# Q·Kᵀ over 96 heads on one core: the later blocks hold eight heads instead of twelve

## The chip, the cores and the metric

The kernel runs on one core of a Trainium2 chip. The metric is the device time of one execution in microseconds (us), lower is better. Three executions of the kernel before gave 1061.80, 1062.16 and 1062.28 us; the median is 1062.16 us.

## The reference

For each of 8 × 12 = 96 heads, a 1024 × 64 matrix Q is multiplied with the transpose of a 1024 × 64 matrix K. Inputs and output are float32.

```python
def reference(q, k):          # q, k: (8, 12, 1024, 64), values 0.1 * randn
    return np.einsum('bhid,bhjd->bhij', q, k).astype(np.float32)   # (8, 12, 1024, 1024)
```

The inputs are 2 × 25.2 MB, the output is 402.7 MB: eight times as much is written as is read.

## The kernel before, in words

The 96 heads are cut into blocks of 2, 2, 4, 8, 8 and six times 12 heads (`sizes`). Within a block, each of Q and K goes through four steps, and then the heads are multiplied one by one.

1. **Load** (`Block.load`, L152 to L163). One DMA brings the float32 rows of all heads of the block into a buffer `x_sb`. Partition p takes the p-th part of the block's rows, which lies in one piece in HBM: 24 KB for twelve heads, 16 KB for eight. There are two `x_sb` buffers, and Q and K take turns, so the next block's Q goes where this block's Q was. Before the DMA is issued, the issuing engine waits until the casts have read the old contents. The loads of the blocks of 2 and 4 heads go to one of the output buffers instead, at the start.
2. **Cast** (`cast_quads`, the instruction at L211). GpSimd turns float32 into fp16, from `x_sb` into one of two buffers `half`. Each of Q and K makes two chunks, so a block has four chunks, and each chunk takes four instructions over 32 partitions.
3. **Transpose** (`transpose_quads`, L230). VectorE transposes a chunk in 32 × 32 squares from `half` into `qT` or `kT`. There are two pairs of `qT` and `kT`, used by blocks in turn. The first transpose of a block waits for the last matmul of the block two before it, which used the same pair. (The first two blocks are transposed by TensorE instead, L244.)
4. **Scores** (`Block.scores`). For each head, TensorE makes 8 × 2 matmuls of 64 × 128 by 64 × 512 (L312) into two halves of PSUM; ScalarE copies each half (128 × 2048 float32, L289) into one of three 4 MB output buffers `o_sb`, four copies a head; SyncE then waits for the fourth copy (L302) and issues one 4 MB store of the head, 32 KB for each partition. ScalarE's first copy into a buffer waits until the store that used the buffer three heads earlier has landed.

All engines' orders are written out by hand in `block()`, L391 to L414. While the heads of block i are multiplied, the four chunks of block i+1 are transposed, one in each quarter of the heads, and each transposed chunk frees a `half` for the next cast. During the same block, ScalarE's queue issues the two loads of block i+2: Q after the second copy of head `n` and K two heads later, where `LOADS` says which heads. Blocks of 12 issue at heads 6 and 8, blocks of 8 at heads 4 and 6, the block of 4 at heads 1 and 3. So the stores are on SyncE's DMA queue, and nearly all loads are on ScalarE's.

```python
    sizes = [2, 2, 4, 8, 8] + [12] * ((BH - 24) // 12)
    CHUNK, HALVES = 96 * 32, 2
    LOADS = {0: (), 1: (), 2: (1, 3), 3: (4, 6), 4: (4, 6)}
```

`CHUNK` is the size of a `half` buffer (elements in a partition), and `self.cut` (L142) is the number of pieces that half of a block's Q must be cut into to fit there; it is 1 in every block.

Of the kernel before, what the change touches and what calls it, by code (L numbers as in the profile page):

```python
# [6 lines left out]
F16 = mybir.dt.float16  # L7
F32 = mybir.dt.float32
P = 128
# [50 lines left out]
def kernel(  # L60
# [8 lines left out]
    B, H, S, D = q.shape  # L69
    NT = S // P  # L70
    BH = B * H
    assert D == 64 and NT == 8 and BH >= 36 and (BH - 24) % 12 == 0

    flat = [x.rearrange("b h s d -> (b h s) d") for x in (q, k)]
    of = out.rearrange("b h i j -> (b h) i j")

    sizes = [2, 2, 4, 8, 8] + [12] * ((BH - 24) // 12)
    PE_BLOCKS, EARLY = 2, 3
    NMAX = max(sizes)
    CHUNK, HALVES = 96 * 32, 2  # L80
    LOADS = {0: (), 1: (), 2: (1, 3), 3: (4, 6), 4: (4, 6)}

    pool = ctx.enter_context(tc.tile_pool(name="sb", bufs=1))
    psum = ctx.enter_context(
# [3 lines left out]
    x_sb = [pool.tile([P, NMAX * S * D // P], F32, name=f"x_sb{i}", tag=f"x{i}") for i in range(2)]  # L88
    half_sb = [pool.tile([P, CHUNK], F16, name=f"half{i}", tag=f"half{i}") for i in range(HALVES)]
    qk_sb = [  # L90
        [pool.tile([P, NMAX * S // 2], F16, name=f"{'qk'[x]}T{i}") for x in range(2)]
        for i in range(2)
    ]
    o_sb = [pool.tile([P, NT, S], F32, name=f"o_sb{i}", tag=f"out{i}") for i in range(3)]
# [27 lines left out]
    n, at = S * D // P * 2, 8 * S // 2  # L122
# [227 lines left out]
    def next_load(eng):  # L350
        if stream:
            b, x = stream.pop(0)
            assert b.i == EARLY or not any(i == b.i - 1 and c[0] == x for i, c in casts)
            b.load(x, eng)
# [20 lines left out]
    def to_half(last):  # L375
        while casts:
            i, c = casts[0]
            if i > last or (blocks[i], c[0]) in stream:
                return
            if not (rooms if i == PE_BLOCKS else halves).free():  # L380
                return
            done = blocks[i].cast_quads(*c)
            if i == 2:
                early_busy[:] = [done]
            casts.pop(0)

    def transposed(b, s):
        b.transpose_quads(*s)
        to_half(b.i)

    def block(i, heads, regions, w):  # L391
        b = blocks[i]
        nxt = blocks[i + 1] if i + 1 < len(blocks) else None
        for n in heads:
            side = {}
            if nxt and nxt.by_pe:
                if n == 1:
                    side = {
                        u: [
                            lambda x=u // 2: nxt.transpose_rows(  # L400
                                x, regions.next(), dve, nc.vector.tensor_copy
                            )
                        ]
                        for u in (1, 3)
                    }
            elif nxt:
                parts = nxt.chunks()
                some = [s for m, s in enumerate(parts) if m * b.N // len(parts) == n]
                side = {0: [lambda s=s: transposed(nxt, s) for s in some]}
            if n in LOADS.get(i, (6, 8)):  # L410
                side[1] = side.get(1, []) + [lambda: next_load(act)]
            b.scores(n, side, regions, w)
            to_half(i + 2 + (n == b.N - 1))
# [8 lines left out]
    for x in range(2):  # L422
        blocks[0].transpose_rows(
            x, quarters.next(), (dve, act)[x], (nc.vector.tensor_copy, nc.scalar.copy)[x]
        )
        to_half(2)
    block(0, [0], quarters, 1)
    halves_ps = Ring([ps_all[:, 2 * S :], ps_all[:, : 2 * S]])
    halves_ps.busy = [quarters.busy[2] + quarters.busy[3], quarters.busy[0] + quarters.busy[1]]
    block(0, [1], halves_ps, 2)  # L430
    for i in range(1, len(blocks)):
        block(i, range(blocks[i].N), halves_ps, 2)
# [31 lines left out]
```

## Time and profile before

| | before |
|---|---|
| time, median of three | 1062.16 us (1061.80 to 1062.28) |
| profiled execution, its span | 1060.4 us (the profile lists no other time of it) |
| TensorE matmul busy | 700.5 us (66%) |
| ScalarE busy | 697.0 us (66%) |
| VectorE busy | 470.6 us (44%) |
| GpSimd busy | 345.3 us (33%) |
| moved by DMA | 453.19 MB, mean 427 GB/s |
| read from and written to HBM | 50.33 MB, 402.65 MB |

The profile is of one execution. Its engines are PE (TensorE), DVE (VectorE), ACT (ScalarE), POOL (GpSimd) and SP (SyncE, which only issues DMAs here); a q behind the name means the engine's own sequencer, for instance while it issues a DMA. The DMA rows count 16 DMA engines that all transfers share: a share of 1.00 or tenths of 9 mean that all sixteen hold a packet nearly all the time. A DMA's packet here is one partition's piece, and q1 and q10 are the queues of SyncE and ScalarE. Behind the DMA rows the trace has a record of each packet (queue, start, duration, size), and of the small completion write that each of the 16 engines makes at the end of each DMA; where the text speaks of packet records, it means these.

### The profile page before, as it was taken

The page shows a single profiled execution, that of the slowest core. Times are in us where ns is not written, and L with a number is a line of the kernel's source. Part 1 is how long each engine was busy: PE and PEld are TensorE (multiplying, and loading weights), DVE is VectorE, ACT ScalarE, POOL GpSimd, SP SyncE. Part 2 cuts the span into 40 slices and gives each one's busy share as a digit, 9 for nine tenths or more (in the row PEclk, how much of TensorE's full clock was granted, in tenths as well). Part 3 has the DMA queues.
Part 4 walks back from the last instruction along what each step waited for, and adds up shares of the span by engine and source line. Part 5 has one row for each costly group of instructions (what it writes and reads, how often), then busy time and mean ns, then how long its engine had stood idle before and what let it go on. Part 6 is the DMA issues. An engine that isn't in the chain of part 4 may idle for free.

```text
span 1060.4 us, 3258 instructions
## 1 busy us (share of the span) xinstructions
PE 700.5 (66%) x1568; PEld 127.3 (12%) x800; DVE 470.6 (44%) x43; ACT 697.0 (66%) x386; POOL 345.3 (33%) x158
## 2 busy tenths in 40 slices
PE   6876755765577557774577855777557777778770
PEld 2111100110111001110011100111001111111110
DVE  2998602991795006960069600795007950000000
ACT  4766755755678557775577755776557777777771
POOL 7667216436360430704307053160531600000000
DMA  9999999999999999999999999999999999999997
GB/s 376 434 435 434 432 419 430 435 428 431 433 432 428 428 435 430 430 431 423 438 431 429 433 431 434 434 429 422 426 432 435 429 434 434 434 435 430 431 434 336
DMA packets 17583, 453.19 MB, mean 427 GB/s; under 512 B 1952, under 2 KB 1952, under 8 KB 2976
## 3 DMA queue, kind: packets, MB, share of 16 engines
q1 hardware_dynamic: 14976, 410.00, 90.0%
q10 hardware_dynamic: 2592, 42.99, 9.7%
q8 instruction: 9, 0.15, 0.0%
q14 instruction: 6, 0.05, 0.0%
HBM read 50.33 MB, written 402.65 MB: 427 GB/s over the span
## 4 chain that ended last, share of the span: by engine, by line
DMA 71%; ACT 17%; PE 7%; DVE 2%; issue 1%; POOL 0%; ACTq 0%; SPq 0%
DMA out_dram<-o_sb 70%; ACT o_sb L289 17%; PE ps_all L312 7%; DVE kT L230 1%; DVE qT L230 1%; DMA o_sb<-in_q_dram 0%; PE ps_all L244 0%; POOL qT L180 0%; DVE kT L251 0%; ACT kT L251 0%; ACTq L36 0%; SPq L168 0%; SPq L459 0%; SPq L97 0%
## 5 line engine op out<-in xcount | busy, mean ns | idle before, releaser
L289 ACT COPY o_sb<-ps_all 128x2048 f32<-128x2048 f32 (+1 forms) x384 | 694.7, 1859 | 333.0 <-DMA out_dram<-o_sb 301.6
L312 PE MATMUL ps_all<-kT,qT 64*128 64x512 f16 x1536 | 696.4, 617 | 327.8 <-ACT o_sb L289 322.4
L211 POOL CAST half<-x_sb 32x3072 f16<-32x3072 f32 (+1 forms) x128 | 323.4, 2527 | 491.6 <-DMA x_sb<-in_q_dram 242.2
L230 DVE STREAM_TRANSPOSE qT<-half 128x3072 f16<-128x3072 f16 (+1 forms) x16 | 222.9, 14132 | 370.0 <-PE ps_all L312 370.0
L309 PEld LDWEIGHTS <-qT 64*128 64x128 f16 x768 | 124.2, 162 | 896.8 <-issue 889.2
L230 DVE STREAM_TRANSPOSE kT<-half 128x3072 f16<-128x3072 f16 (+1 forms) x16 | 224.2, 14217 | 2.8 <-POOL half L211 2.8
L230 DVE STREAM_TRANSPOSE kT<-kT 128x1024 f16<-128x1024 f16 x2 | 9.3, 4836 | 0.0
L230 DVE STREAM_TRANSPOSE qT<-qT 128x1024 f16<-128x1024 f16 x2 | 9.2, 4784 | 0.0
L211 POOL CAST qT<-o_sb 32x1024 f16<-32x1024 f32 x8 | 8.3, 1034 | 1.2 <-DMA o_sb<-in_q_dram 0.8
L211 POOL CAST kT<-o_sb 32x1024 f16<-32x1024 f32 x8 | 8.3, 1033 | 0.5
L251 DVE COPY qT<-ps_all 128x1024 f16<-128x1024 f16 x2 | 2.5, 1225 | 11.0 <-PE ps_all L244 11.0
L289 DVE COPY o_sb<-ps_all 128x1024 f32<-128x1024 f32 x4 | 4.9, 1225 | 4.4 <-PE ps_all L312 4.4
L244 PE MATMUL ps_all<-ident,qT 128*128 128x128 f16 x16 | 2.1, 310 | 6.7 <-POOL qT L180 6.6
L251 ACT COPY kT<-ps_all 128x1024 f16<-128x1024 f16 x1 | 1.0, 1012 | 4.7 <-PE ps_all L244 4.7
L180 POOL CAST qT<-o_sb 128x512 f16<-128x512 f32 x4 | 2.3, 612 | 3.6 <-DMA o_sb<-in_q_dram 3.6
L251 DVE COPY kT<-ps_all 128x1024 f16<-128x1024 f16 x1 | 1.2, 1225 | 4.4 <-PE ps_all L244 4.4
L251 ACT ACT_TABLE_LOAD x1 | 1.3, 1283 | 2.8 <-issue 2.8
L244 PE MATMUL ps_all<-ident,kT 128*128 128x128 f16 x16 | 2.0, 305 | 0.7 <-ACT o_sb L289 0.7
L180 POOL CAST kT<-o_sb 128x512 f16<-128x512 f32 x4 | 2.3, 613 | 0.4 <-DMA o_sb<-in_q_dram 0.4
L244 PEld LDWEIGHTS ps_all<-ident,qT 128*128 128x128 f16 x16 | 1.5, 140 | 6.9 <-POOL qT L180 6.9
L244 PEld LDWEIGHTS ps_all<-ident,kT 128*128 128x128 f16 x16 | 1.5, 136 | 3.3 <-POOL qT L211 1.6
L359 POOL MEMSET ident<- 128x128 f16 x1 | 0.2, 205 | 0.5 <-SPq L97 0.5
(5 smaller groups left out, 0.7 us busy)
## 6 DMA issues: line engine op xcount, KB each, us to landing
out_dram<-o_sb SPq DMA_DIRECT2D x96, 4096.0 KB, 21.7
x_sb<-in_q_dram ACTq DMA_DIRECT2D x6, 3072.0 KB, 22.0
x_sb<-in_k_dram ACTq DMA_DIRECT2D x6, 3072.0 KB, 21.9
x_sb<-in_q_dram SPq DMA_DIRECT2D x1, 2048.0 KB, 14.6
x_sb<-in_k_dram SPq DMA_DIRECT2D x1, 2048.0 KB, 19.6
x_sb<-in_q_dram ACTq DMA_DIRECT2D x1, 2048.0 KB, 18.3
x_sb<-in_k_dram ACTq DMA_DIRECT2D x1, 2048.0 KB, 19.1
o_sb<-in_k_dram ACTq DMA_DIRECT2D x4, 256.0 KB, 4.7
```

Of the source, the lines that this page charges most:

```text
L180: lambda: nc.gpsimd.tensor_copy(out=rows[:, :, h], in_=self.raw[x][:, h * n : (h + 1) * n].rearrange("p (r d) -> p r d", d=D),),
L211: lambda: nc.gpsimd.tensor_copy(out=dst[q0 : q0 + 32].rearrange("p (r d) -> p r d", d=32), in_=raw[32 * b : 32 * b + 32, c * m : (c + 1) * ...
L230: lambda: nc.vector.transpose(out=dst, in_=buf.rearrange("p (r i) -> p r i", i=32)),
L244: lambda: nc.tensor.transpose(t_ps[:, t], rows[:, t], ident),
L251: lambda: copy(out=dst, in_=t_ps.rearrange("c t m -> c m t")), [done]
L289: lambda: (nc.vector.tensor_copy if by_dve else nc.scalar.copy)(out=dst, in_=ps[:, : w * S]),
L309: return nc.tensor.ldweights(stationary, tile_position=(at, 0))
L312: return nc.tensor.add_instruction(mybir.InstMatmult(name=nc.get_next_instruction_name(), ins=[nc.tensor.lower_ap(moving), nc.tensor.lower ...
L359: cleared = gps.run(lambda: nc.gpsimd.memset(ident, 0.0))
```

## The change

All blocks behind the first three hold eight heads: 2, 2, 4 and then eleven times 8. Loads in blocks of 8 go on being issued at heads 4 and 6, which is now the rule for all of them. The buffers `x_sb` and `half` shrink with the largest block; the buffers of `qT` and `kT` keep their size for twelve heads, since the early blocks use their back part as working space (`rooms`).

```diff
-    assert D == 64 and NT == 8 and BH >= 36 and (BH - 24) % 12 == 0
+    assert D == 64 and NT == 8 and BH >= 24 and BH % 8 == 0
...
-    sizes = [2, 2, 4, 8, 8] + [12] * ((BH - 24) // 12)
+    sizes = [2, 2, 4] + [8] * ((BH - 8) // 8)
     PE_BLOCKS, EARLY = 2, 3
     NMAX = max(sizes)
-    CHUNK, HALVES = 96 * 32, 2
-    LOADS = {0: (), 1: (), 2: (1, 3), 3: (4, 6), 4: (4, 6)}
+    CHUNK, HALVES = 64 * 32, 2
+    LOADS = {0: (), 1: (), 2: (1, 3)}
...
     qk_sb = [
-        [pool.tile([P, NMAX * S // 2], F16, name=f"{'qk'[x]}T{i}") for x in range(2)]
+        [pool.tile([P, 12 * S // 2], F16, name=f"{'qk'[x]}T{i}") for x in range(2)]
...
-            if n in LOADS.get(i, (6, 8)):
+            if n in LOADS.get(i, (4, 6)):
                 side[1] = side.get(1, []) + [lambda: next_load(act)]
```

## The prediction

> **What bounds the kernel now.** I began with the DMA rows of the page, because the busy shares of the engines (66% at most) name no bound.
>
> ```profile
> DMA  9999999999999999999999999999999999999997
> DMA packets 17583, 453.19 MB, mean 427 GB/s; under 512 B 1952, under 2 KB 1952, under 8 KB 2976
> q1 hardware_dynamic: 14976, 410.00, 90.0%
> q10 hardware_dynamic: 2592, 42.99, 9.7%
> DMA 71%; ACT 17%; PE 7%; DVE 2%; issue 1%; POOL 0%; ACTq 0%; SPq 0%
> ...
> out_dram<-o_sb SPq DMA_DIRECT2D x96, 4096.0 KB, 21.7
> x_sb<-in_q_dram ACTq DMA_DIRECT2D x6, 3072.0 KB, 22.0
> ...
> x_sb<-in_q_dram ACTq DMA_DIRECT2D x1, 2048.0 KB, 18.3
> x_sb<-in_k_dram ACTq DMA_DIRECT2D x1, 2048.0 KB, 19.1
> ```
>
> The sixteen DMA engines are full from the first slice to the last: 90.0% for the queue of the stores (and the first loads), 9.7% for the other loads. The chain of waits, in a stretch without and one with loads, says what each costs:
>
> ```profile
> 334.91 29.09 DMA out_dram<-o_sb
> ...
> 371.55 29.21 DMA out_dram<-o_sb
> ...
> 408.60 21.21 DMA out_dram<-o_sb
> ...
> 891.20 21.72 DMA out_dram<-o_sb
> ...
> 920.47 21.72 DMA out_dram<-o_sb
> ```
>
> One step is three heads, because there are three output buffers. Late, without loads, it takes 920.47 - 891.20 = 29.27 us, 9.76 us for a 4 MB store. From 334.91 to 408.60, two steps with one 3 MB load each, it is 73.69 us, so two loads cost 73.69 - 58.54 = 15.15 us. A store lands 21.7 us after its issue, over two store times, so the queue holds another store whenever one ends. Time is made of what the DMA engines do per byte, per DMA and in slow packets; nothing else counts until it empties that queue.
>
> **The change part by part.** The change of instructions does what its words say: 18 loads of 16 KB a partition stand where 12 of 24 KB were (blocks 5 to 10 become 5 to 13); matmuls, copies and stores are the same in number, and SyncE's order is unchanged.
>
> *Bytes.* 12 × 3 MB = 18 × 2 MB. Nothing.
>
> *Six more DMAs, 768 more packets.* The packet records give 1213 ns as the commonest duration of a 32 KB packet, 912 ns for 24 KB, 611 ns for 16 KB. That is linear, with some 9 ns a packet beyond the bytes. On each of 16 engines, 12 × 8 × 912 ns = 87.6 us becomes 18 × 8 × 611 ns = 88.0 us: +0.4 us. The spacing of completion writes includes the DMA's end: 9.68 us for a 4 MB store, and 4.89 us for a 2 MB load at the start. Twice the second less the first is 0.10 us for each DMA whatever its size, hence +0.6 us for six. I take +0.6, which is measured on whole DMAs; +0.4 is the low end. As to the high end, the 256 KB loads land 4.7 us after issue; if each added load stood alone and held everything for that time it would be 28 us. It cannot be so while the queue is full, as at these loads.
>
> The Trainium skill, "DMA: Bandwidth & Descriptors", section "Anatomy of one DMA", speaks against the change: it fits a DMA (on GpSimd's path) as about 2.0 us fixed plus its bytes over 436 GB/s; by that, an estimate is 6 × 2.0 = 12 us more if the fixed part were paid in line. The trace disagrees as long as the queue is full: 0.10 us a DMA.
>
> *Slow packets.* Some packets take 60 to 1200 ns over the commonest duration of their size, and they crowd into the first 10 us of a load, of Q above all, in the load's own and in the stores' packets. Summed over both queues and divided by 16 engines, the six pairs of 3 MB loads (from 140, 240, 340, 480, 600 and 740 us) have 0.7, 0.4, 0.7, 0.8, 0.4 and 1.0 us, 4.0 us in all. The one pair of 2 MB loads that runs beside stores, 60 to 120 us, has 0.08 us. The windows over such pairs and over a free stretch show the same, roughly:
>
> ```profile
> 62.50:111.50 49.00, 31.37 (x71) 5.56 (x35) 45.09 (x6) 30.07 (x17) 36.98 (x21) 1.00 1.00 433
> 345.50:399.50 54.00, 28.96 (x66) 5.19 (x32) 0.00 (x0) 29.08 (x16) 21.92 (x8) 1.00 1.00 430
> 610.00:664.00 54.00, 29.06 (x64) 5.20 (x32) 0.00 (x0) 29.20 (x17) 21.92 (x8) 1.00 1.01 433
> 862.00:1030.00 168.00, 125.26 (x277) 22.37 (x138) 1.15 (x1) 123.60 (x68) 0.00 (x0) 1.00 1.00 432
> ```
>
> (Last columns: share of the DMA engines, GB/s.) If 16 KB pieces have no slow packets, -4.0 us; if they come once for each pair, nine pairs instead of six make +2.0; if they go by bytes, 0. But the end is not set by the mean engine. The sixteen completion writes of the last store are spread over 5.3 us, and the last engine is one that has lost about 0.08 us in every store of the load-free stretch, while it lost only some 0.9 us over all six load stages beyond that. On this engine the ends are -0.9 and +0.45 us. I take 0: one pair of 2 MB loads is thin evidence for none, and the early pair on SyncE's queue (20 to 40 us, no stores beside) has 0.6 us of slow packets at 16 KB.
>
> *Casts, transposes, issues.*
>
> ```profile
> L211 POOL CAST half<-x_sb 32x3072 f16<-32x3072 f32 x96 | 263.0, 2740 | 467.4 <-DMA x_sb<-in_q_dram 238.6 <-DVE qT L230 224.0
> L230 DVE STREAM_TRANSPOSE kT<-half 128x3072 f16<-128x3072 f16 x12 | 187.0, 15797 | 0.0
> L211 POOL CAST half<-x_sb 32x2048 f16<-32x2048 f32 x32 | 60.4, 1887 | 24.3 <-DVE qT L230 13.0 <-DMA x_sb<-in_k_dram 6.1 <-DMA x_sb<-in_q_dram 3.5
> L230 DVE STREAM_TRANSPOSE qT<-half 128x2048 f16<-128x2048 f16 x4 | 37.3, 9503 | 1.1 <-PE ps_all L312 1.1
> ```
>
> And the list of waits:
>
> ```profile
> ACT o_sb L289 <- DMA out_dram<-o_sb: 301.6, 89, 8.3
> ```
>
> POOL: 176 × 1.887 = 332 us instead of 323. DVE: 44 × 9.49 = 418 us instead of 447. Both lie beside stores: a block of eight lasts 8 × 9.68 + 2 × 4.89 = 87 us, its four transposes 4 × 9.5 = 38 us, its sixteen casts 30 us, so the next block is ready some 49 us early; cover gone, POOL's +9 us would be the price. ACT issues six more loads at 0.33 us (its row), 2 us, beside 301.6 us in which it waits for stores; uncovered, +2. The wait before an issue is for casts that ended long before: the last cast of K follows the block's second transpose (19 us) and takes 7.5 us, so it is over 27 us into the block, and K's load comes at head 6, some 60 us in. Queued behind that wait are ACT's copies, for which PE and then SyncE's stores wait; none of it moves. Q's load, 18 us to landing, is through when K's is issued 24 us later; K's lands about 2 us into the next block, where its first transpose comes 19 us in. Late next, if anything, is that K. Smaller `x_sb` and `half` free SBUF that nothing uses: nothing.
>
> *Sum.* The profiled span, 1060.4 us, is 1.8 us under the median of the runs, which I keep as what lies around the span. 1060.4 + 0.6 + 0 = 1061.0 us of span, so 1062.8 us.
>
> **The rivals.**
>
> *A, the forecast: all hidden.* Full queue, +0.6 us, slow packets as before on the engine that ends last: 1062.8, between 1061.5 (no slow packets, low price: +0.4 - 0.9) and 1063.6. For it: the shares of 1.00 in all windows. Against: it hangs on the one slow engine staying the last.
>
> *B, faster: 16 KB pieces have no slow packets, and all engines gain.* -4.0 + 0.6 = -3.4 us: 1058.8. For it: 0.08 against 0.4 to 1.0 us a pair. Against: a single pair, and the last engine has only 0.9 us to give. It decides from 2.7 us of recovered time on the last engine, which needs that engine's steady loss to be smaller in the timed runs than in the profiled one.
>
> *C, slower, the other side: slow packets come with each load's beginning.* Nine pairs instead of six, on the engine that ends last as on the mean one: +2.0 + 0.6 = 2.6 us: 1064.8. It decides from 1.5 us more in slow packets. For it: they crowd at the beginnings of loads. Against: the 2 MB pair.
>
> *D, slower: a new wait empties the queue of stores.* The place is the first matmul of a block, which waits for the transposes. When a store lands, two more are queued, 19.4 us, and refilling the freed buffer takes 1.9 + 1.9 + 3.6 = 7.4 us in the chain, so the stores run 12 us ahead. If K came late by more than the 49 + 12 = 61 us, each of the nine blocks would lose the rest: 1 us each gives 1071.8. For it: a block has a third less time. Against: its work shrinks likewise, and the eight-head block that stands in the trace has no such wait.
>
> *E, slower: the fixed part of a DMA is paid.* A 256 KB load lands 4.7 us after its issue, and its 8 packets on an engine take 8 × 84 ns = 0.7 us; if the sixteen engines stood still for the other 4.0 us at each of six added loads, it would be 24 us: 1086.8 with A's 0.6. Every window with loads has a DMA share of 1.00, which is against it. By the Trainium skill's figure above, in place of this one, it would be about 1074.
>
> **How the numbers follow.** A 0.48, B 0.26, C 0.18, D 0.06, E 0.02. The prediction is A's, 1062.8 us. A's own range is 1061.5 to 1063.6. The range reaches to B's and C's times with the 0.2 us by which the two prices of a DMA differ, 1058.6 to 1065.0, and leaves out D, E and the outer parts of B and C. Within 0.2% of the median, 2.1 us, is what cannot well be told from no change: A is there (0.48); faster is B (0.26); slower are C, D and E (0.26).
>
> **What would show it.** Right: q10 with 768 more packets of data (and 96 completion writes) at about the same share; a DMA share of 1.00 in windows over every pair of loads; a late three-head step of 29.3 us; two steps with a load each at about 58.5 + 9.8 us; casts and transposes over long before their block starts. B would show as slow packets of less than 1 us over all nine later pairs of loads; C as 6 us; D as long waits of PE for DVE at L312; E as slices of the DMA row below 9. I am wrong if the slow packets have another cause than the loads' shape, for instance the place in HBM, which moves with the blocks too, or if the slow engine of this execution is not there in others.

## The result, and the profile after

The changed kernel takes 1066.29 us (median, 1065.72 to 1067.06) beside 1062.22 us before in the same comparison: a ratio of 1.0037, 95% interval 1.0025 to 1.0048, or +4.1 us with +2.7 to +5.1 as its interval. The forecast was no change (1062.8 us); the time lies 1.3 us above its range, which ended at 1065.0 us, and 1.5 us above rival C's 1064.8 us. The profiled execution has a span of 1064.6 us (before: 1060.4), and its own time is 1066.41 us, so 1.8 us lie around the span again.

The page of the changed kernel, its DMA rows (the columns are as before):

```profile
DMA  9999999999999999999999999999999999999997
GB/s 374 433 433 434 434 433 430 433 419 432 432 429 422 437 434 425 432 433 414 430 433 424 426 433 433 422 432 434 425 425 432 424 429 432 431 433 433 433 433 316
q1 hardware_dynamic: 14976, 410.00, 89.9%
q10 hardware_dynamic: 3456, 42.99, 9.6%
...
x_sb<-in_q_dram ACTq DMA_DIRECT2D x10, 2048.0 KB, 19.7
x_sb<-in_k_dram ACTq DMA_DIRECT2D x10, 2048.0 KB, 19.7
```

The engines are full as before, the bytes are the same, and q10 has 864 more records: 768 packets of data and 96 completion writes. Only the rate dips, more often than before, to 414 to 426 GB/s.

The chain of waits (start and length in us), two steps with a load each and late ones without:

```profile
394.77 26.64 DMA out_dram<-o_sb
...
428.96 26.98 DMA out_dram<-o_sb
...
463.50 21.48 DMA out_dram<-o_sb
...
895.24 21.50 DMA out_dram<-o_sb
...
924.30 21.50 DMA out_dram<-o_sb
...
953.35 21.48 DMA out_dram<-o_sb
982.38 23.00 DMA out_dram<-o_sb
1012.94 21.41 DMA out_dram<-o_sb
```

A step without loads is 29.06 us, 0.2 us less than the 29.27 us before, which fits with the engine that was last before and lost 0.08 us in each store. The step from 982.38 to 1012.94 is an exception, 30.56 us; more on it below. The two steps with loads take 463.50 - 394.77 = 68.73 us, so two loads cost 10.6 us for 9.6 us of bytes (8 × 602 ns for each at the packets' slope). Nine later pairs pay such a surplus instead of six.

The groups of instructions and the waits:

```profile
L211 POOL CAST half<-x_sb 32x2048 f16<-32x2048 f32 x176 | 332.1, 1887 | 547.5 <-DMA x_sb<-in_q_dram 348.8
L230 DVE STREAM_TRANSPOSE qT<-half 128x2048 f16<-128x2048 f16 x22 | 204.1, 9466 | 463.4 <-PE ps_all L312 463.4
```

```profile
ACT o_sb L289 <- DMA out_dram<-o_sb: 305.8, 89, 6.3
PE ps_all L312 <- DVE kT L230: 3.0, 1, 3.0
```

Casts cost what was worked out (332 us), transposes a little less (410 us in their two rows, instead of 418), and no block waits for them: PE's matmuls wait for these transposes once, 3.0 us, in this kernel and in the one before. Rival D, a new wait, is out, and so is E.

Windows of 50 us over the early pair of 2 MB loads, over four of the nine later pairs, and a late stretch without loads (last columns: DMA share, GB/s):

```profile
62.50:111.50 49.00, 31.44 (x71) 5.59 (x35) 45.10 (x6) 30.09 (x17) 36.95 (x21) 1.00 1.01 434
...
310.00:360.00 50.00, 29.06 (x65) 5.19 (x32) 8.03 (x1) 29.09 (x17) 15.09 (x8) 1.00 1.00 426
...
488.00:538.00 50.00, 29.41 (x66) 5.32 (x33) 9.31 (x2) 29.45 (x17) 15.09 (x8) 1.00 1.01 424
...
752.00:802.00 50.00, 29.64 (x67) 5.29 (x33) 8.89 (x1) 29.68 (x17) 15.09 (x8) 1.00 1.00 425
840.00:890.00 50.00, 29.07 (x65) 5.18 (x32) 8.21 (x1) 29.11 (x17) 15.09 (x8) 1.00 1.00 424
910.00:1040.00 130.00, 97.10 (x215) 17.15 (x106) 8.74 (x1) 97.04 (x54) 0.00 (x0) 1.00 1.00 433
```

The early pair loses nothing, in this kernel too; the four later pairs shown, of the same 2 MB loads, lose about 2%, and the other five 1 to 2% (424 to 429 GB/s).

**Where the 4.2 us of span went.** The packet records give three terms. The slow packets (all that packets of both queues took beyond the commonest duration of their size, divided by 16) rose from 6.1 to 8.6 us over the whole run, +2.5 us; behind the first 60 us of the records, where the later loads are, from 4.7 to 7.4 us. The mean of the sixteen completion writes of the last store came 2.9 us later (1051.2 us behind the first load's completion before, 1054.2 after), which leaves 0.4 us for the six added DMAs. And the last of the sixteen engines was 5.0 us behind the mean one instead of 3.5: +1.5 us. Together 4.4 us; the span grew by 0.2 us less, since less of it lies behind the last completion.

Most of the third term does not come from a load. In the store ahead of 982 us the last engine was 3.8 us behind the mean one, 0.3 us more than at the end of the kernel before. The step at 982 us, with no load near, takes 30.56 us where its neighbours take 29.03 to 29.06, and the packet records have one instruction fetch at 981.84 us: a single packet of 16 KB, 961 ns long, on one of the sixteen engines. The kernel before has its fetch at 978.56 us, but its steps show nothing of it:

```profile
979.02 21.72 DMA out_dram<-o_sb
1008.30 21.72 DMA out_dram<-o_sb
```

So the fetch there ran on an engine that was not the last. Such a long step about 980 us, 1.4 to 1.7 us over its neighbours, stands in seven of nine profiles with 18 loads (this one and eight from the experiments below) and in none of the four with 12 (at most 0.8 us there). Whether that is chance is not shown.

### The profile page after: what moved, and what is told of

Its sections match the earlier page's. It is cut to its first block, busy times and chain, and to the rows that moved or that the text cites. A ratio compares the mean times of both kernels' runs of the same rounds, so it can differ in the third digit from the quotient of the medians.

```text
span 1064.6 us, 3333 instructions
## 1 busy us (share of the span) xinstructions
PE 700.6 (66%) x1568; PEld 127.3 (12%) x800; DVE 432.7 (41%) x55; ACT 697.1 (65%) x386; POOL 353.9 (33%) x206
## 4 chain that ended last, share of the span: by engine, by line
DMA 71%; ACT 17%; PE 7%; DVE 2%; issue 1%; POOL 0%; ACTq 0%; SPq 0%
DMA out_dram<-o_sb 71%; ACT o_sb L289 17%; PE ps_all L312 7%; DVE kT L230 1%; DVE qT L230 1%; DMA o_sb<-in_q_dram 0%; PE ps_all L244 0%; POOL qT L180 0%; DVE kT L251 0%; ACT kT L251 0%; ACTq L36 0%; SPq L168 0%; SPq L459 0%; SPq L97 0%
## 5 line engine op out<-in xcount | busy, mean ns | idle before, releaser
L211 POOL CAST half<-x_sb 32x2048 f16<-32x2048 f32 x176 | 332.1, 1887 | 547.5 <-DMA x_sb<-in_q_dram 348.8
L230 DVE STREAM_TRANSPOSE qT<-half 128x2048 f16<-128x2048 f16 x22 | 204.1, 9466 | 463.4 <-PE ps_all L312 463.4
L230 DVE STREAM_TRANSPOSE kT<-half 128x2048 f16<-128x2048 f16 x22 | 205.9, 9551 | 2.9 <-POOL half L211 2.9
## 6 DMA issues: line engine op xcount, KB each, us to landing
x_sb<-in_q_dram ACTq DMA_DIRECT2D x10, 2048.0 KB, 19.7
x_sb<-in_k_dram ACTq DMA_DIRECT2D x10, 2048.0 KB, 19.7
```

Source lines behind the costliest of these rows:

```text
L211: lambda: nc.gpsimd.tensor_copy(out=dst[q0 : q0 + 32].rearrange("p (r d) -> p r d", d=32), in_=raw[32 * b : 32 * b + 32, c * m : (c + 1) * ...
L230: lambda: nc.vector.transpose(out=dst, in_=buf.rearrange("p (r i) -> p r i", i=32)),
```

## The experiments

Each kernel was measured beside the kernel before on the same chip. "Slow" is the sum of slow packets behind the first 60 us, and "mean end" and "last" are the mean engine's end and how far the last engine is behind it, all three from the packet records of one profiled execution. Loads are counted that begin beside stores, behind the early pair.

| kernel | later loads × piece | slow, us | mean end, us | last, us | time, us | ratio, 95% interval |
|---|---|---|---|---|---|---|
| before | 12 × 24 KB | 4.7 | 1051.2 | 3.5 | 1062.4 | |
| changed | 18 × 16 KB | 7.4 | 1054.2 | 5.0 | 1066.3 | 1.0025 to 1.0048 |
| changed, again | 18 × 16 KB | 6.6 | 1054.0 | 6.6 | 1066.4 | 1.0025 to 1.0050 |
| pair at once | 18 × 16 KB | 7.2 | 1054.1 | 6.0 | 1066.5 | 1.0028 to 1.0053 |
| same place | 18 × 16 KB | 7.5 | 1054.1 | 4.0 | 1065.5 | 1.0023 to 1.0048 |
| 16 KB, 24 KB apart | 18 × 16 KB | 7.6 | 1054.6 | 4.8 | 1066.3 | 1.0020 to 1.0046 |
| 16 KB, 17 KB apart | 18 × 16 KB | 7.6 | 1054.9 | 4.9 | 1067.2 | 1.0031 to 1.0061 |
| GpSimd busy | 18 × 16 KB | 7.7 | 1054.5 | 4.0 | 1066.0 | 1.0024 to 1.0055 |
| VectorE busy | 18 × 16 KB | 6.2 | 1053.3 | 5.0 | 1065.9 | 1.0022 to 1.0049 |
| changed, early loads | 18 × 16 KB | 7.3 | 1054.2 | 4.9 | 1066.3 | 1.0024 to 1.0051 |
| before, loads behind stores | 12 × 24 KB | 4.9 | 1051.8 | 4.2 | 1064.9 | 1.0014 to 1.0032 |
| 24 KB, 32 KB apart | 12 × 24 KB | 5.1 | 1051.3 | 4.0 | 1062.4 | 0.9988 to 1.0008 |
| before, early loads | 12 × 24 KB | 4.8 | 1051.8 | 3.4 | 1062.9 | 0.9994 to 1.0012 |
| blocks of ten | 14 × 20 KB | 5.8 | 1052.7 | 3.8 | 1064.3 | 1.0006 to 1.0024 |
| blocks of six | 24 × 12 KB | 7.9 | 1054.7 | 3.4 | 1065.5 | 1.0024 to 1.0049 |
| loads in two halves | 36 × 8 KB | 5.9 | 1053.3 | 4.9 | 1065.5 | 1.0018 to 1.0044 |
| blocks of four | 38 × 8 KB | 4.7 | 1052.4 | 6.1 | 1065.0 | 1.0017 to 1.0037 |

**Do the slow packets come where reading begins?** The first theory, rival C made sharper, was that each stretch of reading beside stores pays once.

```diff
-            if n in LOADS.get(i, (4, 6)):
-                side[1] = side.get(1, []) + [lambda: next_load(act)]
+            loads = LOADS.get(i, (4, 4))
+            if n in loads:
+                side[1] = side.get(1, []) + [
+                    lambda: next_load(act) for _ in range(loads.count(n))
+                ]
```

> The changed kernel, but K's load is issued right behind Q's at head 4 instead of two heads later: nine pairs of loads make nine stretches of reading beside stores instead of eighteen. Theory S (slow packets come where reading begins, about 0.39 us for each beginning, from 6.9 us over 18 later loads in the changed kernel's packet records): nine beginnings fewer, -3.5 us against the changed kernel, about 1062.8 us. Rival D (each DMA pays its own beginning, back to back or not): 1066.3 us. Rival Y (slow packets go by bytes read): 1066.3 us, too, with the slow packets spread over the whole of the loads.

Nothing was won: 1066.5 us. The page of this kernel shows that the loads did follow one another, K landing 15 us behind Q:

```profile
x_sb<-in_q_dram ACTq DMA_DIRECT2D x10, 2048.0 KB, 20.0
x_sb<-in_k_dram ACTq DMA_DIRECT2D x10, 2048.0 KB, 34.7
```

So it is not the stretch of reading that pays; eighteen loads in nine stretches have as many slow packets (7.2 us) as in eighteen. The plain theory falls. (The pause that this run takes away is short, since Q landed 19.7 us after its issue and K was issued about 24 us after Q; the opposite case, Q and K four heads apart, is below.)

```diff
-    sizes = [2, 2, 4] + [8] * ((BH - 8) // 8)
+    sizes = [2, 2, 4, 8] + [4] * ((BH - 16) // 4)
...
-    LOADS = {0: (), 1: (), 2: (1, 3)}
+    LOADS = {0: (), 1: (), 3: (4, 6)}
...
-            if n in LOADS.get(i, (4, 6)):
+            if n in LOADS.get(i, (1, 3)):
```

> Blocks of 2, 2, 4, 8 and then twenty times 4: 40 loads of 1 MB (8 KB a partition) on ScalarE's queue where the changed kernel has 20 of 2 MB. Theory S: 20 more beginnings at 0.39 + 0.10 us, +9.7 us against the changed kernel, about 1076 us. Rival Y (by bytes): only 20 x 0.10 us more, 1068.3 us.

1065.0 us, under both numbers and far under the theory's. A load of 8 KB pieces has only 0.09 us of slow packets on the mean engine, against 0.37 us for the 16 KB pieces of the changed kernel and 0.32 us for the 24 KB pieces of the one before. (These prices per load count packets over 60 ns too slow, from 3 us before a load's first packet to 1 us behind its last.)

**Is it the two queues taking turns?** The loads of block 5 and later go to SyncE's queue, between stores.

```diff
-                side[1] = side.get(1, []) + [lambda: next_load(act)]
+                side[1] = side.get(1, []) + [lambda: next_load(sp if i >= EARLY else act)]
```

> The kernel before (blocks of 12), but the loads of block 5 and later are issued on SyncE's queue, between two stores, instead of on ScalarE's: no two queues to take turns between. Theory S in its plain form (a read that begins beside running stores costs something, from whatever queue): 1062.2 us, as before. Rival Q (the slow packets come from taking turns between two queues): the 4.0 us of slow packets over the six pairs are gone on the mean engine, about 1058 to 1060 us.

```profile
x_sb<-in_q_dram SPq DMA_DIRECT2D x6, 3072.0 KB, 29.3
x_sb<-in_k_dram SPq DMA_DIRECT2D x6, 3072.0 KB, 36.7
```

The loads now wait their turn (29 and 37 us to landing instead of 22), and the slow packets stay, 4.9 us. Rival Q falls. The time even rose, to 1064.9 us; the profiled execution took 1063.3 us, the lowest time of this kernel, and its records do not show where the other 1.6 us of the median lie. That is left open.

**Is it the place, or the distance of the pieces?** First, every load of block 5 and later reads block 4's rows.

```diff
-            src = flat[x][self.first * S : (self.first + self.N) * S]
+            first = min(self.first, blocks[4].first) if self.i > 4 else self.first
+            src = flat[x][first * S : (first + self.N) * S]
```

> The changed kernel, but every load of block 5 and later reads the rows of block 4 (heads 8 to 15) again, whose own loads had no slow packets; so the output from head 16 on is that of other heads. Theory S: 1066.3 us, slow packets as in the changed kernel. Rival P (the place in HBM decides): slow packets fall to about 0.1 us a pair, -6 us, about 1060 us.

7.5 us of slow packets and 1065.5 us, so the place does not decide. Second, the distance between the pieces that neighbouring partitions read; `96` is 24 KB, `68` is 17 KB, and in the kernel before `128` is 32 KB.

```diff
-            src = flat[x][self.first * S : (self.first + self.N) * S]
+            pitch = 96 if self.i > 4 else self.R
+            at = min(self.first * S, BH * S - P * pitch)
+            src = flat[x][at : at + P * pitch]
...
-                out=self.raw[x], in_=src.rearrange("(p r) d -> p (r d)", p=P)
+                out=self.raw[x],
+                in_=src.rearrange("(p r) d -> p (r d)", p=P)[:, : self.elems],
```

> The changed kernel, but each partition's 16 KB piece of a load of block 5 and later is read at a distance of 24 KB from the next one's instead of 16 KB (as in the kernel before), so other rows are read and the output from head 16 on is not the reference's. Theory L (the sixteen DMA engines begin to read in step, at places that lie 4 pieces apart, and 64 KB apart is worse than 96 KB): slow packets beyond 60 us fall from 7.4 us on the mean engine to about 4.5 us, time about 1063 us. Rival Z (the piece's size or the load's number decides, not its places): slow packets stay at 7.4 us, about 1066 us.

> As the run with a distance of 24 KB, but with 17 KB between the beginnings of two 16 KB pieces, so that engines that read in step are 68 KB apart, no power of two. Theory L: slow packets of 4.5 us or less on the mean engine, time about 1063 us or less. Rival Z: 7.4 us, about 1066 us.

> The kernel before with its 24 KB pieces read at a distance of 32 KB instead of 24 KB for block 5 and later (other rows, so the output from head 24 on is not the reference's). Theory L: slow packets rise from 4.7 us on the mean engine to 7 us or more, time about 1065 us. Rival Z: 4.7 us, 1062.4 us.

All three went Z's way: 7.6 and 7.6 us of slow packets for the 16 KB pieces, 5.1 for the 24 KB pieces, and times of the kernel with the same number of loads. Neither the place nor the distance of what is read makes the slow packets. Where the pieces are written in SBUF was not varied by itself.

**Halves.** Each 2 MB load as two DMAs, back to back, each with 8 KB of every partition's 16 KB.

```diff
-            dma = eng.eng.dma_start(
-                out=self.raw[x], in_=src.rearrange("(p r) d -> p (r d)", p=P)
-            )
+            rows = src.rearrange("(p r) d -> p (r d)", p=P)
+            parts = 2 if self.i > 4 else 1
+            m = self.elems // parts
+            for c in range(parts):
+                dma = eng.eng.dma_start(
+                    out=self.raw[x][:, c * m : (c + 1) * m],
+                    in_=rows[:, c * m : (c + 1) * m],
+                )
...
```

> The changed kernel, but each 2 MB load of block 5 and later is issued as two DMAs back to back, each with 8 KB of every partition's 16 KB, still 16 KB apart. Theory L: slow packets stay at about 7.4 us, and 18 more DMAs add about 1 to 2 us, 1067 to 1068 us. Rival Z, by the size of the pieces (8 KB pieces cost 4.7 us over all loads in the run with blocks of four): slow packets fall to about 4.7 us, 1065 us.

5.9 us, between the two, and 1065.5 us. With blocks of four it says that 8 KB pieces are cheap by load (0.14 and 0.09 us), though there are 36 and 38 of them.

**Is it the idle engines beside the load?** In the records of the kernels so far, Q's loads had most of the slow packets, and GpSimd and VectorE sat idle as they began, while GpSimd cast Q as K's loads began. So the changed kernel was given needless copies on GpSimd, and then on VectorE, right behind each load, and both kernels were run with their loads moved to where VectorE transposes.

```diff
+    def load_beside_work():
+        next_load(act)
+        event = [(act, act.count)]
+        for _ in range(14):
...
+                lambda: nc.gpsimd.tensor_copy(out=idle_dst, in_=idle_src),
...
-                side[1] = side.get(1, []) + [lambda: next_load(act)]
+                side[1] = side.get(1, []) + [load_beside_work if i > 2 else lambda: next_load(act)]
```

> The changed kernel, plus work for GpSimd that nothing needs: right after each load issued in block 3 or later, 14 copies of 128 x 1024 float32 from one scratch buffer to another, so that GpSimd is busy while the load begins. Theory W (packets are slow where a load begins while GpSimd and VectorE are both idle: in the records, loads that begin beside a busy GpSimd or VectorE have 0 to 0.3 us of slow packets on the mean engine, the others 0.25 to 0.9): the nine loads of Q lose their 0.45 us, slow packets fall from 7.4 us on the mean engine to about 3 us, time about 1062 us. Rival V (what matters is that Q's load comes after a long stretch without reading and K's soon after Q's): slow packets stay at 7.4 us, about 1066 us.

> The same with VectorE in GpSimd's place: 14 copies of 128 x 1024 float32 right after each load issued in block 3 or later. Theory W: slow packets fall to about 3 us on the mean engine or less, since both loads of a pair begin beside a busy engine, time about 1062 us. Rival V: 7.4 us, about 1066 us.

```diff
-    LOADS = {0: (), 1: (), 2: (1, 3), 3: (4, 6), 4: (4, 6)}
+    LOADS = {0: (), 1: (), 2: (1, 3), 3: (1, 3), 4: (1, 5)}
...
-            if n in LOADS.get(i, (6, 8)):
+            if n in LOADS.get(i, (1, 5)):
```

> The kernel before with its loads earlier in the block, where VectorE transposes: heads 1 and 5 in blocks of twelve (and in the second block of eight), 1 and 3 in the first block of eight, instead of 6 and 8, and 4 and 6. Theory W: both loads begin beside a busy VectorE, slow packets fall from 4.7 us on the mean engine to about 1 us, time about 1059 us. Rival V: Q and K now both come after four heads or more without reading, so K's loads cost as much as Q's, slow packets rise to about 7 us, about 1065 us.

```diff
-            if n in LOADS.get(i, (4, 6)):
+            if n in LOADS.get(i, (1, 3)):
```

> The changed kernel with its loads at heads 1 and 3 of each block instead of 4 and 6, where VectorE transposes. Theory W: slow packets fall from 7.4 us on the mean engine to about 2 us, time about 1061 us. Rival V: the distance between Q's and K's load is as before, slow packets stay at 7.4 us, about 1066 us.

The beginnings of three of Q's loads, 12 us each, in windows of the changed kernel, where GpSimd (the column ahead of the clock) is idle:

```profile
310.00:322.00 12.00, 7.15 (x16) 1.31 (x8) 0.00 (x0) 5.83 (x4) 0.00 (x0) 1.00 0.99 410
488.00:500.00 12.00, 6.23 (x14) 1.14 (x7) 0.00 (x0) 5.83 (x4) 0.00 (x0) 1.00 1.00 408
840.00:852.00 12.00, 6.96 (x16) 1.30 (x8) 0.00 (x0) 5.63 (x4) 0.00 (x0) 1.00 0.98 404
```

and in the kernel with copies on GpSimd:

```profile
310.00:322.00 12.00, 7.16 (x16) 1.30 (x8) 0.00 (x0) 5.93 (x4) 9.77 (x10) 1.00 0.97 403
488.00:500.00 12.00, 6.24 (x15) 1.04 (x7) 0.00 (x0) 6.26 (x5) 10.93 (x11) 1.00 0.98 411
840.00:852.00 12.00, 6.95 (x16) 1.29 (x8) 0.00 (x0) 6.21 (x4) 9.97 (x10) 1.00 0.98 406
```

403 to 411 GB/s against 404 to 410, and 433 without a load: a busy GpSimd changes nothing that shows, and the slow packets of the whole run are 7.7 us. VectorE's copies left 6.2 us of slow packets, a little under the changed kernel's own 6.6 and 7.4 and far from 3. Theory W falls in all four runs. Rival V falls as well, in the kernel before with early loads: Q and K are four heads apart there, and the slow packets stay at 4.8 us, not 7.

**By the number of loads, or is 16 KB dear in itself?** What was left is that whatever is done to 12 loads or to 18, the slow packets follow their number. Blocks of ten lie between the two kernels, blocks of six beyond; the changed kernel ran along.

```diff
-    sizes = [2, 2, 4] + [8] * ((BH - 8) // 8)
+    sizes = [2, 2, 4, 8] + [10] * ((BH - 16) // 10)
...
-    CHUNK, HALVES = 64 * 32, 2
-    LOADS = {0: (), 1: (), 2: (1, 3)}
+    CHUNK, HALVES = 80 * 32, 2
+    LOADS = {0: (), 1: (), 2: (1, 3), 3: (4, 6)}
...
-            if n in LOADS.get(i, (4, 6)):
+            if n in LOADS.get(i, (5, 7)):
```

For blocks of six, `sizes` is `[2, 2, 4, 8, 8] + [6] * ((BH - 24) // 6)`, `CHUNK` stays, `LOADS` also has `4: (4, 6)`, and the other blocks load at heads 3 and 5.

> The changed kernel once more, beside the next two on one chip: 1066.3 us, 7.4 us of slow packets on the mean engine, whichever theory holds.

> Blocks of 2, 2, 4, 8 and eight times 10: 16 later loads of 2.5 MB with 20 KB pieces, between the 12 of the kernel before and the 18 of the changed one. Theory N (each load costs the same 0.39 us of slow packets while its pieces are larger than some size, and 0.65 us in the time measured, a sixth of the 3.9 us between the two kernels): 6.3 us of slow packets on the mean engine, 1062.4 + 4 x 0.65 = 1065.0 us. Rival T (16 KB pieces are dear in themselves): slow packets near 4.9 us, 1062.8 us.

> Blocks of 2, 2, 4, 8, 8 and twelve times 6: 24 later loads of 1.5 MB with 12 KB pieces. Theory N, if 12 KB is still above that size: 24 x 0.39 = 9.4 us of slow packets on the mean engine, 1062.4 + 12 x 0.65 = 1070.2 us. Rival R (a load's price falls with its pieces below 16 KB, to 0.12 us at 8 KB, so about 0.25 us at 12 KB): 6 us of slow packets, 1064 to 1066 us.

Blocks of ten: 1064.3 us (interval 1063.0 to 1064.9), between the kernels; T's 1062.8 is just outside, N's 1065.0 just above. The expectation counted 16 loads, but two of them are the early pair, which costs little in any kernel (0 to 0.3 us a load); 14 loads are two more than before, and N's 0.65 us and 0.39 us each then give 1063.7 us, inside the interval, and 5.5 us of slow packets; 5.8 were measured, against T's 4.9. Blocks of six: 1065.5 us and 7.9 us of slow packets; a load of 12 KB pieces has 0.29 us, between R's 0.25 and N's 0.39, and N's 1070 us is wrong. In slow packets it lies between the two, in time it is R's.

In short, a load has 0.30 to 0.34 us of slow packets on the mean engine with 24 and 20 KB pieces, 0.29 to 0.38 with 16 KB, 0.29 with 12 KB, 0.09 to 0.14 with 8 KB. Between 12 and 24 KB it is a price of the load (or of its eight packets on each engine, which cannot be told apart here), not of its bytes. It is a mean, though: in the kernel before, Q's loads have 0.54 us each and K's 0.09, in the changed kernel 0.46 and 0.28. Every kernel loads Q and K in equal number, so a price of the pair cannot be told from one of the load either. The run with blocks of ten is the only one between 12 and 18 loads, and its interval is near T's number, so this rests as much on the nine profiles with 18 loads, none of which came below 6.2 us, and the four with 12, none of which came above 5.1. And it is a price in slow packets: the time does not follow the number of loads beyond 18 (24 loads of 12 KB pieces, 1065.5 us; 38 of 8 KB, 1065.0 us).

No version ran faster than the kernel before.

## Why the prediction was wrong, point by point

- *What bounds the kernel*: right. The DMA engines are full, a late step stays at 29 us but for the one with the fetch, and the engines off the DMA path changed much as worked out, without a new wait.
- *Bytes, and six more DMAs*: right, and a little dear. +0.6 us was taken; the mean end less the slow packets shows 0.4, the low end.
- *The fixed 2.0 us for a DMA that the Trainium skill gives ("DMA: Bandwidth & Descriptors", section "Anatomy of one DMA")*: the page's fit is for DMAs issued by GpSimd, these loads are ScalarE's, and the trace went on disagreeing with carrying it over; 0.4 us for six DMAs is 0.07 us each. The slow packets make the whole price of a load larger than that, but not 2 us.
- *Slow packets, "I take 0"*: this step failed. Its ends on the mean engine were -4.0 and +2.0 us; the value was +2.5, since nine pairs pay a little more each (0.74 us) than six did (0.63). Two readings misled. The one pair of 2 MB loads beside stores seemed to speak for no slow packets at 16 KB; it has none in the changed kernel either, while the same 2 MB loads later have 0.4 us each. The row nearest in shape was the wrong one; the six late 3 MB pairs, nearest in circumstances, were right.
- *"The end is not set by the mean engine", -0.9 to +0.45 us on the last one*: this step failed too, and turned a mechanism that was seen into no change. An engine that loses 0.08 us in each store is in the changed kernel too, but it ended only 1.9 us behind the first. (The records do not name the engine; it is told by how packets follow one another.) Another was last: it lost 3.8 us against the first one during the load stages, and 1.4 us more in the step at 982 us, the one with the fetch. So the loss of one engine hid nothing. How far the last engine is behind the mean one was 3.4 to 4.2 us in four profiles with 12 loads and 4.0 to 6.6 in nine with 18, but it does not follow the slow packets: blocks of six have 3.4 us with 7.9 us of slow packets, blocks of four 6.1 with 4.7. Beyond the fetch, what sets it stays open.
- *The range of A*: its ends do not come out of the terms named. 0.4 - 0.9 us from 1062.2 is 1061.7 us, not 1061.5, and 0.6 + 0.45 is 1063.2, not 1063.6. The stated range does not rest on them.
- *Rival C*, with 0.18, had the main term: nine pairs instead of six, +2.0 us and a DMA price, 1064.8 us. It missed 1.5 us, mainly by taking the last engine to lose no more than the mean one. Its reason, that slow packets come with each load's beginning, is not shown: 36 and 38 loads with 8 KB pieces have fewer slow packets than 18 with 16 KB. *Rival B* had the sign wrong: 16 KB pieces have as many slow packets in a load as 24 KB pieces, so with more loads there are more.

## What to carry to other kernels

When a kernel is bound by full DMA engines, the same bytes in half as many again loads are not free: here 18 instead of 12 loads beside stores cost 4 us, 0.65 us each, of which a view of busy shares or of bytes shows nothing. It is no fixed price: 24 loads cost 3.1 us and 38 loads 2.6 us more than 12, with smaller pieces. To price one more transfer, take the surplus of transfers that run under the same circumstances (late, beside a full store queue), not of the one that has the right size but ran early. And where sixteen engines finish a program together, ask for the last of them, and in more than one trace: a loss that hides behind the one engine that is last in one trace shows in another, where a different engine is last.

## What was not expected of the hardware

- A load beside stores slows the packets of the stores, ahead of its own first packet: in the changed kernel about a third of the slow packets (2.4 of 6.8 us, counting those over 60 ns) are the one store packet directly ahead of a load's first packet on each engine. Slow packets come whatever the queue, the place read, the distance of the pieces and the work of GpSimd and VectorE. Why, and why 8 KB pieces are cheap and the first pair, at 60 to 110 us, is nearly free (0 to 0.3 us a load, nothing in most profiles), is not settled.
- The sixteen DMA engines, given equal bytes, drift 5 to 10 us apart by the end of a millisecond, and one of them lost 0.08 us in each 4 MB store of the kernel before for no reason that the trace names. The step in which one 16 KB instruction fetch runs (961 ns in the changed kernel) is 1.5 us longer there than its neighbours.
